# Three pads that move tiles in SBUF, in an encoder layer with a gating unit, a long convolution and a ConvGLU

## The chip, the cores and the metric

The kernel runs on one core of one Trainium2 chip. The metric is the device time of one execution in microseconds, as the median of several runs; less is better. TensorE (PE) multiplies matrices from SBUF into PSUM banks; its weight loads are listed apart, as PEld. VectorE (DVE), ScalarE (ACT) and GpSimd (POOL) do the rest of the arithmetic, SyncE (SP) issues most DMAs. SBUF has 128 partitions; an address here is a byte within a partition.

## The reference

One layer over 512 tokens of width 2048, in float32:

```python
h = rms_norm(x, norm1_g);  p = h @ w_in                      # 2048 -> 5120
zu = gelu(p[:, :1024]);    zv = rms_norm(gelu(p[:, 1024:2048]), sgu_norm_g)
y_a = zu * (sgu_w[head] @ zv + sgu_b)                        # in chunks of 128 tokens
x0, x1, v = dwconv3(p[:, 2048:])                             # three times 1024
u = v * x1;  y_b = x0 * (bidir_long_conv(u, k) + d * u)      # k from a small MLP, through FFTs
x = x + concat(rms_norm(y_a), rms_norm(y_b)) @ w_out
gv = rms_norm(x, norm2_g) @ ffn_w_up                         # 2048 -> 2 * 5504
x = x + (gelu(dwconv3(gv[:, :5504])) * gv[:, 5504:]) @ ffn_w_down
return rms_norm(x, final_g)
```

## The kernel before

Every large product is computed exactly from float32 by three products of a narrower type (`fp32r`): an operand is split into a high part and a rest, `exact_pair` (lines 130 to 132, ScalarE casts, VectorE subtracts), and `mm3` (lines 169 to 172) adds high x high, rest of the moving operand x high, high x rest of the weights into one PSUM bank. `PE.matmul(o, weights, moving)` loads 128 x 128 weights and then streams the moving operand, mostly 512 columns of 4 bytes.

The weights come in units of two K tiles by 512 columns through three buffers each of `raw`, `hi` and `lo` (pool `wp`); `next_unit` keeps the DMA three units and the split two units ahead. The stages, in order:

- projections of h by `w_in` (`projA`, banks `pa`): hi and lo are the weights, hH and hL (the two parts of x times its gain, `split_x`) are moving. 4 feature tiles x 16 K tiles x 3 products are a group of 192 matmuls. For the value branch (`projB`, banks `pv`) the roles are exchanged: hH and hL are weights, hi and lo moving.
- beside them the filter of the long convolution (`filter_pieces`; banks `fh`, `fw`, `fx`; tiles of the pool `mlp`, called `fm`) and the spatial gating unit (`sgu_pieces`, banks `sg`).
- the long convolution in four chunks (`forward`, `products`, `spectra`, `inverse`; banks `fw`, `iv`) woven into the first half of the output projection (`out_group`, banks `po`). Moving there are yh and ylo, the two parts of the gated branch, and in the second half ybH and ybL.
- the FFN in 11 groups of four feature tiles (the last of three): gate and value projections of h2H and h2L (banks `pa`, function `hk` gives the tile), then the down projection (`down`, banks `pd`) with aH and aL moving. Its four blocks of 48 matmuls use the same four banks, which VectorE empties into `xacc` (line 1048). The last group is done in token halves (banks `pl`, 256 columns).

The order is the one in which the code is written, on every engine. A tile's address comes from its pool: pools on the left are stacked upwards from the bottom of SBUF, pools on the right downwards from the top. Left are `const`, `wp`, then in the stack `left` the pool `yl` (au, then ylo; line 220) and, once the filter's pools are closed, `y` (line 647: u and ybH; zH, zL, x0 and ybL; yh). Right are `A` (hH, hL), later `long`, and `A2` and `A3` (h2H, h2L). When `left` is closed, the pool `ffn` (aH, aL) begins where `yl` began.

Of the kernel before, what the change touches and what calls it, by code (L numbers as in the profile page):

```python
# [12 lines left out]
F32 = mybir.dt.float32  # L13
# [4 lines left out]
P = 128  # L18
# [12 lines left out]
CC = 256  # L31
# [11 lines left out]
def encoder_kernel(ctx: ExitStack, tc: tile.TileContext, a: dict, out: bass.AP):  # L43
# [16 lines left out]
    def bank(name):  # L60
        """one of the four banks of the streamed products"""
        return psum.tile([P, 512], F32, tag="mm", name=name, bufs=4)

    def sbank(name):
        """one of the four banks of everything that runs between them"""
        return psum.tile([P, 512], F32, tag="sd", name=name, bufs=4)
# [9 lines left out]

    # ---------------------------------------------------------------- the stream of weights
    # a unit: rows k0*128.. of a weight, nk K tiles by nc_ columns
    plan = []
# [22 lines left out]
    for g in range(2):  # L102
        plan_proj(w_in, 2 * CB + g * 512, 4)
    # beside the long convolution half of the low parts are computed on Pool
    on_pool = set()
# [12 lines left out]
    def load_raw(key):  # L118
        src, k0, nk, c0, n = key
        raw = wp.tile([P, 2, 512], F32, tag="raw", name="raw", bufs=3)  # L120
        rows = src[k0 * P : (k0 + nk) * P, c0 : c0 + n].rearrange("(k p) c -> p k c", p=P)
        if st_["dma"] == 0:
            # the first one in halves, as the products wait for it
            for k in range(nk):
                SP.dma_start(raw[:, k : k + 1, :n], rows[:, k : k + 1, :])
        else:
            SP.dma_start(raw[:, :nk, :n], rows)
        return raw
# [27 lines left out]
    def next_unit(key):  # L156
        """the exact fp32r pair of the next unit; the two after it are already on their way"""
        i = st_["use"]
        assert plan[i][1:] == key[1:] and plan[i][0] is key[0], (i, key)
        split_to(i + 3)  # L160
        dma_to(i + 4)
        st_["use"] += 1
        return split_units.pop(i)
# [9 lines left out]

    # ---------------------------------------------------------------- x and constants
    right = ExitStack()
# [42 lines left out]

    left = ExitStack()
    ylp = pool("yl", stack=left)  # L220

# [3 lines left out]
    def rsqrt(r, ss, n):  # L225
        """r = (ss / n + eps) ** -0.5"""
        DVE.tensor_scalar(r, ss, 1.0 / n, EPS, ALU.mult, ALU.add)
        POOL.tensor_tensor(r, r, nhalf.broadcast_to(list(r.shape)), ALU.pow)

    def rms_col(acc, n, name):  # L230
        """squares, to be summed over the partitions too -> 1/rms, [token, 1] per tile of tokens"""
        nt = acc.shape[-1] // P
        o = sbank("mc")
        for t in range(nt):
            PE.matmul(o[:, t : t + 1], acc[:, t * P : (t + 1) * P], ones[:, 0:1], start=True, stop=True)
        r = const.tile([P, NT], F32, tag="rc", name=name, bufs=3)
        rsqrt(r[:, :nt], o[:, :nt], n)
        return r

    def row_of(r, name, nt=NT):  # L240
        """[token, 1] columns -> the same row of tokens on all partitions"""
        o = sbank("mr")
        for t in range(nt):
            PE.matmul(o[:, t * P : (t + 1) * P], r[:, t : t + 1].broadcast_to([P, P]), ident, start=True, stop=True)
        row = const.tile([P, L], F32, tag="rb", name=name, bufs=2)
        ACT.copy(row[:, : nt * P], o[:, : nt * P])
        return row
# [22 lines left out]

    # ---------------------------------------------------------------- implicit filter
    khat_d = dram.tile([NCC, P, 4 * 2 * CC], F32, name="khat_d")
# [5 lines left out]
    zT, fw1 = zw[:, :L], zw[:, L:]  # L278
    # the last layer comes out twice, on both halves of the partitions
    fw2 = fm.tile([FO, 3 * FO], F32, name="fw2")  # L280
# [23 lines left out]

    # features of the lags: rows 0..63 the high parts, 64..127 the low parts
    h3 = fm.tile([P, L], F32R, name="h3")
    h0 = fm.tile([P, P], F32R, name="h0")

    def mlp_out():
        h = hcur[-1]  # L310
        t = fm.tile([P, L], F32R, name="h3t")
        ACT.copy(t, h)
        ACT.copy(h3[:FO, :], h[:FO, :])
        DVE.tensor_tensor(h3[FO:, :], h[FO:, :], f32(t[FO:, :]), ALU.subtract)
        # the backward half has no tap at lag 0
        DVE.tensor_copy(h0, f32(h3[:, :P]))
        DVE.tensor_scalar(h0[:, 0:1], f32(h0[:, 0:1]), 0.0, None, ALU.mult)
# [5 lines left out]
    def forward_mm(cs, tab, rH, rL):  # L323
        """cos (0) or sin (1) sums of the four token phases [tok, CC] -> banks [128, 2, CC] of phases 0 1, 2 3"""
        Hs, Ls = tab
# [10 lines left out]
    def butterfly(G, U, T):  # L336
        """phase sums (U: 0+2, 1+3; T: 0-2, 1-3) [P, cs, 2, CC] -> frequencies f + 256 j:
        G[:, i, cs, m] holds j = 2 i + m"""
        DVE.tensor_tensor(G[:, 0, :, 0, :], U[:, :, 0, :], U[:, :, 1, :], ALU.add)
# [12 lines left out]
    def filter_pieces(tab):  # L352
# [31 lines left out]
        for c in range(NCC):  # L384
# [35 lines left out]

            # the sum of both directions goes with cos and their difference with sin;
            # the odd phases, which the frequencies f + 256 and f + 768 turn by a quarter, need both
            def turned(cs, tab, rH, rL):
# [45 lines left out]

    # ---------------------------------------------------------------- projections  # L470
    def projA(src, c0, nf, done, rhs=None):
        """[feature, token] tiles of h @ src[:, c0 : c0 + nf*128]; done(ps) takes them out of the banks"""
        ps = [bank("pa") for _ in range(nf)]
# [31 lines left out]

    # value branch, [token, feature]
    gv = [[None] * 2 for _ in range(NT)]
# [23 lines left out]
    def eo(ap):  # L531
        """[P, 512] stored by token modulo 4, seen in token order"""
        return ap.rearrange("p (r m) -> p m r", r=4)
# [3 lines left out]

    # centred depthwise convolutions over tokens (free axis)
    def conv3(pl, ps, r, names, fb, to=None):
        """to: where the result goes, by token modulo 4; without it, in token order in a passing tile"""  # L540
        w0, w1, w2_, b = (lambda i, n=n: col(*n(fb + i)) for n in names)
# [47 lines left out]
    def go_to(n):  # L589
        """emit the products up to K tile n of the projections"""  # L590
        while pos[0] < n:
            next(main)
            pos[0] += 1

    # a_u, with the rest of x and the filter behind its K tiles
    fgen = filter_pieces((tabH, tabL))
# [48 lines left out]
    fs.close()  # L645

    yps.append(pool("y", stack=left))
    yp = yps[0]
    ms = ExitStack()
    mp = pool("mix", side="right", stack=ms)  # L650
    go_to(47)
    # spatial gating weights, transposed: [j, h, i]
    sb = mp.tile([P, NH, P], F32, name="sb")
# [109 lines left out]

    # ---------------------------------------------------------------- long conv and output projection
    keep = ExitStack()
# [41 lines left out]
    def turn(c):  # L807
        """[channel, token] -> [token, channel] pair of u"""
        H, Lo = spl("uH"), spl("uL")
# [182 lines left out]

    # ---------------------------------------------------------------- ConvGLU
    fst = ExitStack()
# [74 lines left out]

    # ---------------------------------------------------------------- the last group, and the final norm  # L1070
    # token halves, so that the first half leaves while the second is computed
    a2s.close()
# [35 lines left out]
    def rms3():  # L1108
        """1/rms per token from tiles of squares"""
        ms_ = [sbank("ms") for _ in range(nt)]  # L1110
# [16 lines left out]
    for th in range(2):  # L1127
        hs = slice(th * HW, (th + 1) * HW)
        # sums of squares: two running ones; at the end the last tiles go to the tensor engine as they are
        accs = [lp_.tile([P, HW], F32, tag=f"ss{i}", name=f"ss{i}", bufs=2) for i in range(2)]  # L1130
# [41 lines left out]
def shape_constants():  # L1172
    """Tables that depend on the sequence length and widths alone."""
    perm = np.concatenate([np.arange(r, L, 4) for r in range(4)])
# [10 lines left out]
    win = np.ascontiguousarray(win.reshape(NT, P, CB).transpose(1, 0, 2))  # L1185
    # transforms of 1024 points at frequencies f + 1/2: forward [m, r, cos/sin, f] for token 4 m + r,
    # inverse [f, parity e, cos/sin, kt, (q m)] for frequency f + 256 kt and token 4 m + 2 q + e
    i = np.arange(P)
# [9 lines left out]

# the vectors that are used as per-partition columns, in one array
_VECS = [  # L1200
# [19 lines left out]
def laid_out(inputs, zT):  # L1220
    """The inputs as the kernel reads them: the same numbers, some of them transposed or packed."""
    g = {n: np.ascontiguousarray(inputs[n]) for n in _INS}
# [30 lines left out]
```

## Time and profile before

| | us |
|---|---|
| median of 3 runs | 2259.96 |
| lowest and highest run | 2259.07, 2260.71 |
| span of the profiled execution, from its first to its last instruction | 2257.4 |
| TensorE busy in it | 2189.7 |
| VectorE, ScalarE, GpSimd busy | 1133.1, 671.9, 317.5 |
| mean granted TensorE clock | 0.982 |

The profiled execution is told by its span; the runs were timed apart from it. A listed duration of a matmul runs from its start to a modelled end and overlaps the next matmul, so a sum of durations is no time; the distance of two starts is. "Idle" is time of an engine before an instruction, with what ended it.

### The profile page before, as it was taken

Reading aid. Unit: us, or ns where it says so; the run is one execution under the profiler, and the core shown is the slowest. Engines: PE = TensorE matmul, PEld = TensorE weight load, DVE = VectorE, ACT = ScalarE, POOL = GpSimd, SP = SyncE. Lnnn points to the kernel's source line nnn. Section 1 sums busy time; section 2 is a strip of 40 time slices with the busy share of each in tenths; the row PEclk is TensorE's granted clock in tenths of the full one; section 3 lists DMA queues with packets and bytes.
Section 4 is the critical chain, followed back from the end, with each engine's and each line's share of the span. In section 5 each row is a group of like instructions: output and inputs, shape, how many; then the busy total and the mean of one; then the engine's idle time right before and its main releaser. Section 6 shows DMA issues by size and latency. Waiting matters only on the chain.

```text
span 2257.4 us, 23811 instructions
## 1 busy us (share of the span) xinstructions
PE 2189.7 (97%) x9742; PEld 1782.5 (79%) x9742; DVE 1133.1 (50%) x1320; ACT 671.9 (30%) x851; POOL 317.5 (14%) x201
## 2 busy tenths in 40 slices
PE   7999999999888999999999999999999999999997
PEld 5778887778777888787887878878787887878877
DVE  8664465556676853534336353443534335343456
ACT  5333432222343332222122221222222122221333
POOL 5221121001344520101001010000101001010003
PEclk9999999999898999999999999999999999999998
DMA  6333223243212423222322323222222222222332
GB/s 208 99 109 122 85 87 92 83 131 111 86 66 93 140 93 96 93 92 94 102 95 93 94 92 95 91 96 94 94 92 95 93 94 93 93 94 85 95 120 75
DMA packets 113480, 223.10 MB, mean 99 GB/s; under 512 B 7035, under 2 KB 18491, under 8 KB 111580
## 3 DMA queue, kind: packets, MB, share of 16 engines
q1 hardware_dynamic: 109184, 215.69, 29.5%
q10 hardware_dynamic: 4188, 5.90, 0.8%
q8 instruction: 76, 1.25, 0.2%
q14 instruction: 32, 0.26, 0.0%
HBM read 213.18 MB, written 8.39 MB: 98 GB/s over the span
## 4 chain that ended last, share of the span: by engine, by line
PE 84%; DVE 10%; issue 2%; POOL 1%; DMA 1%; ACT 1%; SPq 0%; DVEq 0%; POOLq 0%; ACTq 0%
PE pa L170 19%; PE pa L172 19%; PE pa L171 19%; PE pd L170 5%; PE pd L172 5%; PE pd L171 5%; DVE cv L559 2%; DVE lo L132 1%; PE po L170 1%; PE po L171 1%; PE po L172 1%; PE pv L170 1%; PE pv L171 1%; PE pv L172 1%; DVE ev L546 1%
## 5 line engine op out<-in xcount | busy, mean ns | idle before, releaser
L132 DVE TENSOR_TENSOR lo<-raw,hi 128x1024 fp32r<-128x1024 f32 (+2 forms) x369 | 462.6, 1256 | 899.5 <-ACT hi L131 899.4
L131 ACT CAST hi<-raw 128x1024 fp32r<-128x1024 f32 (+2 forms) x369 | 382.3, 1036 | 1156.1 <-PE pa L171 738.2
L170 PE MATMUL pa<-h2H,hi 128*128 128x512 f32 x1376 | 543.6, 395 | 0.0
L172 PE MATMUL pa<-h2H,lo 128*128 128x512 f32 x1376 | 543.4, 395 | 0.0
L171 PE MATMUL pa<-h2L,hi 128*128 128x512 f32 x1376 | 543.4, 395 | 0.0
L172 PEld LDWEIGHTS pa<-h2H,lo 128*128 128x128 f32 x1376 | 258.4, 188 | 62.5
L170 PEld LDWEIGHTS pa<-h2H,hi 128*128 128x128 f32 x1376 | 258.4, 188 | 62.4
L171 PEld LDWEIGHTS pa<-h2L,hi 128*128 128x128 f32 x1376 | 258.4, 188 | 62.4
L170 PE MATMUL pd<-aH,hi 128*128 128x512 f32 x640 | 249.8, 390 | 14.8 <-DVE xacc L1048 14.8
L172 PE MATMUL pd<-aH,lo 128*128 128x512 f32 x640 | 249.2, 389 | 0.0
L171 PE MATMUL pd<-aL,hi 128*128 128x512 f32 x640 | 249.1, 389 | 0.0
L1011 POOL TENSOR_TENSOR gg<-gg,r 128x512 f32<-128x512 f32 x43 | 73.9, 1723 | 1243.8 <-ACT gg L1010 1243.8
L172 PE MATMUL pa<-hH,lo 128*128 128x512 f32 x512 | 206.2, 403 | 6.0 <-DVE lo L132 6.0
L170 PE MATMUL pa<-hH,hi 128*128 128x512 f32 x512 | 207.5, 405 | 1.2 <-DVE ev L546 1.2
L171 PE MATMUL pa<-hL,hi 128*128 128x512 f32 x512 | 205.8, 402 | 0.0
L170 PEld LDWEIGHTS pd<-aH,hi 128*128 128x128 f32 x640 | 120.1, 188 | 43.6 <-ACT hi L131 17.2
L172 PEld LDWEIGHTS pd<-aH,lo 128*128 128x128 f32 x640 | 120.1, 188 | 25.1
L171 PEld LDWEIGHTS pd<-aL,hi 128*128 128x128 f32 x640 | 120.1, 188 | 24.9
L1048 DVE TENSOR_TENSOR xacc<-xacc,pd 128x512 f32<-128x512 f32 x160 | 106.0, 685 | 42.4 <-PE pd L172 42.4
L172 PEld LDWEIGHTS pa<-hH,lo 128*128 128x128 f32 x512 | 98.7, 193 | 32.7 <-DVE lo L132 8.1
L170 PEld LDWEIGHTS pa<-hH,hi 128*128 128x128 f32 x512 | 99.0, 193 | 29.1 <-DVE ev L546 4.2
L171 PEld LDWEIGHTS pa<-hL,hi 128*128 128x128 f32 x512 | 98.6, 193 | 22.0
(243 smaller groups left out, 2305.1 us busy)
## 6 DMA issues: line engine op xcount, KB each, us to landing
raw<-in_ffn_w_up SPq DMA_DIRECT2D x160, 512.0 KB, 3.5
raw<-in_ffn_w_down SPq DMA_DIRECT2D x84, 512.0 KB, 3.5
raw<-in_w_in SPq DMA_DIRECT2D x79, 512.0 KB, 3.6
raw<-in_w_out SPq DMA_DIRECT2D x32, 512.0 KB, 3.5
raw<-in_ffn_w_up SPq DMA_DIRECT2D x16, 384.0 KB, 3.2
khat_d<-kh SPq DMA_DIRECT2D x4, 1024.0 KB, 3.9
kh<-khat_d SPq DMA_DIRECT2D x4, 1024.0 KB, 4.8
res<-in_xT SPq DMA_DIRECT2D x4, 1024.0 KB, 4.7
```

Of the source, the lines that this page charges most:

```text
L131: ACT.copy(hi, src)
L132: eng.tensor_tensor(lo, src, f32(hi), ALU.subtract)
L170: PE.matmul(o, ah, bh, start=start, stop=False)
L171: PE.matmul(o, ah, bl, start=False, stop=False)
L172: PE.matmul(o, al, bh, start=False, stop=stop)
L546: DVE.tensor_tensor(eo(e), pairs(o), pairs(r), ALU.mult)
L559: DVE.scalar_tensor_tensor(dd, e[:, from_ : from_ + z_ - a_], w(f), dd, ALU.mult, ALU.add)
L1011: POOL.tensor_tensor(g_, g_, r2[0], ALU.mult)
L1048: DVE.tensor_tensor(x_, x_, o, ALU.add)
```

## The change

The change opens three pools that nothing reads or writes:

```diff
+    def pad(name, nbytes, side=None, stack=None):
+
+        pool(name, side=side, stack=stack).tile([P, nbytes // 4], F32, name=name)
+
+    pad("padr", 1152, "right")
     right = ExitStack()
     Apool = pool("A", side="right", stack=right)
...
     left = ExitStack()
+    pad("padl", 32, stack=left)
     ylp = pool("yl", stack=left)
...
     fs.close()
 
+    pad("padu", 32, stack=left)
     yps.append(pool("y", stack=left))
```

The rest of the diff drops comments and docstrings, so line numbers shift. `padr` stays for the whole program: every tile on the right lies 1152 bytes lower. `padl` and `padu` live as long as the stack `left`, up to the FFN: `yl` and the filter's tiles lie 32 bytes higher, `y` and what is stacked on it 64 bytes. `const` and `wp` stay, and so do the tiles of `ffn`, which is opened after `left` is closed. On every engine the same instructions stand in the same order. Four waits name another instruction, because tiles of a later pool cover other old ones: VectorE's for the rest part of the inverse table (invL), ScalarE's for its first squares after the residual sum, and GpSimd's for the second and third product of gg.

Where the operands of the matmuls start, in bytes modulo 512 (a weight tile is taken in steps of 512 bytes, a moving tile in steps of 1024 or 2048, so this is the same for each matmul of a row):

| matmul | moving, before | weights, before | moving, after | weights, after |
|---|---|---|---|---|
| pa from hH, hL | 480 | 352 (hi, lo) | 352 | 352 |
| pv | 352 (hi, lo) | 480 (hH, hL) | 352 | 352 |
| po from yh | 352 | 352 (hi, lo) | 416 | 352 |
| po from ylo | 352 | 352 (hi, lo) | 384 | 352 |
| po from ybH, ybL | 352 | 352 (hi, lo) | 416 | 352 |
| pa from h2H, h2L | 480 | 352 (hi, lo) | 352 | 352 |
| pd from aH, aL | 352 | 352 (hi, lo) | 352 | 352 |
| pl (256 columns) | 352 (aH, aL) | 480 (lH, lL) | 352 | 352 |
| iv (256 columns) | 352 (invH, invL) | 480 (sH, sL) | 416 | 352 |
| fw in the convolution (256) | 480 (uH, uL) | 352 (tabH, tabL) | 352 | 416 |
| fw, fx in the filter (256) | 352 (kH, kL) | 352 (tabH, tabL) | 384 | 384 |
| sg (256) | 480 (w2) | 352 (zH, zL) | 352 | 416 |

Modulo 2048, 480 is 2016 for hH, hL, h2H and h2L, and 352 is 864 for hi, lo, aH, aL, yh, ylo, ybH and ybL and, after, for hH, hL, h2H and h2L. Of the pool `y` the yh tiles end at byte 127840 before; h2H3, the lowest h2 tile, starts at 126944, and the other h2 tiles lie between 135136 and 196576.

## Rows read from the trace of the kernel before

**Rows 1.** The page: busy time by engine; the chain that ended last, by engine.
```profile
PE 2189.7 (97%) x9742; PEld 1782.5 (79%) x9742; DVE 1133.1 (50%) x1320; ACT 671.9 (30%) x851; POOL 317.5 (14%) x201
...
PE 84%; DVE 10%; issue 2%; POOL 1%; DMA 1%; ACT 1%; SPq 0%; DVEq 0%; POOLq 0%; ACTq 0%
```

**Rows 2.** Windows: stretch, its us; busy us and instructions by engine; clock, DMA, GB/s.
```profile
0.00:47.00 47.00, 34.09 (x111) 22.90 (x112) 41.05 (x42) 30.90 (x47) 27.93 (x20) 0.93 0.66 230
...
564.00:717.00 153.00, 128.50 (x650) 111.04 (x650) 98.16 (x109) 58.96 (x71) 59.13 (x36) 0.88 0.22 77
966.50:1055.50 89.00, 89.00 (x383) 71.58 (x382) 26.77 (x29) 19.54 (x21) 0.00 (x0) 1.00 0.30 95
332.00:532.00 200.00, 198.35 (x848) 158.99 (x847) 105.83 (x136) 57.17 (x64) 13.66 (x8) 1.00 0.33 102
```

**Rows 3.** Groups of TensorE by form: names, shape, count; busy us, mean ns; idle before.
```profile
L170 PE MATMUL pa<-h2H,hi 128*128 128x512 f32 x1376 | 543.6, 395 | 0.0
...
L170 PE MATMUL pd<-aH,hi 128*128 128x512 f32 x640 | 249.8, 390 | 14.8 <-DVE xacc L1048 14.8
...
L170 PE MATMUL fw<-kH,tabH 128*128 128x256 f32 x32 | 9.0, 282 | 0.0
L170 PE MATMUL fw<-uH,tabH 128*128 128x256 f32 x32 | 9.0, 281 | 0.0
```

**Rows 4.** Instructions on the tile hi: duration ns min/median/max; first and last start us.
```profile
L170 PE MATMUL pa<-h2H,hi x1376: 390/393/478, 785.5 to 2157.3; 128*128 128x512 f32 x197
...
L170 PE MATMUL pd<-aH,hi x640: 387/389/468, 921.2 to 2202.3; 128*128 128x512 f32 x160
```

**Rows 5.** Timeline of TensorE in the FFN: start us, duration us, instruction, idle before.
```profile
1068.60 0.47 PE L170 MATMUL pd<-aH,hi 128*128 128x512 f32 x1 [1.57 <-DVE xacc L1048]
1068.91 0.40 PE L171 MATMUL pd<-aL,hi 128*128 128x512 f32 x1
...
1101.36 0.40 PE L170 MATMUL pa<-h2H,hi 128*128 128x512 f32 x1
...
1190.95 0.39 PE L170 MATMUL pd<-aH,hi 128*128 128x512 f32 x1
```

**Rows 6.** Timeline of TensorE: first and last start of an unbroken run in other stages.
```profile
198.54 0.39 PE L171 MATMUL pv<-lo,hH 128*128 128x512 f32 x1
...
251.06 0.40 PE L172 MATMUL pv<-hi,hL 128*128 128x512 f32 x1
...
399.44 0.40 PE L171 MATMUL pa<-hL,hi 128*128 128x512 f32 x1
...
443.59 0.40 PE L172 MATMUL pa<-hH,lo 128*128 128x512 f32 x1
...
585.43 0.39 PE L170 MATMUL po<-yh,hi 128*128 128x512 f32 x1
...
601.57 0.39 PE L172 MATMUL po<-yh,lo 128*128 128x512 f32 x1
```

**Rows 7.** Timeline of TensorE: 24 matmuls of 256 columns, and the one behind.
```profile
576.90 0.29 PE L170 MATMUL iv<-invH,sH 128*128 128x256 f32 x1
...
579.79 0.40 PE L170 MATMUL po<-yh,hi 128*128 128x512 f32 x1
```

**Rows 8.** Waits of TensorE: who for whom; us in total, times, longest us.
```profile
PE pd L170 <- DVE xacc L1048: 14.8, 10, 1.6
PE iv L170 <- ACT sH L131: 14.4, 4, 4.3
```

## The prediction

> **What bounds the kernel now.** I read the page's busy line and chain first, then the windows by stage, then the groups of matmuls, and last the start times of single matmuls. TensorE is busy 97% of the span and carries 84% of the chain that ended last [rows 1]. By stage [rows 2] only two stretches are not TensorE's: the first 47 us (it is busy for 34.1 of 47 us while x and the first weights arrive) and the long convolution, 564 to 717 us (128.5 of 153 us; the clock is at 0.88 of full there because of the idle spells). In the projections TensorE is busy throughout, at full clock in the two windows shown, while VectorE and ScalarE are at 53% and 29% (332 to 532 us) or 30% and 22% (966.5 to 1055.5 us), and DMA at about 30%. So what counts is the pitch of the matmuls, from one start to the next. No instruction is added, removed or moved by this change; only addresses move.
>
> The pitch is not one number. I take it from start times, since the listed duration of a matmul overlaps the next one. In the FFN [rows 5] the 384 projection matmuls (two groups of 16 K tiles x 4 feature tiles x 3) from 1101.36 to 1190.95 us take 89.59 us, 233.3 ns each. In the down projection the 143 steps from 1068.91 to 1101.36 us take 32.45 us, 226.9 ns each. Shape, type, weights' buffers and clock are the same. The other stages fall into the same two classes [rows 6]: pv, 226 steps, 52.52 us, 232.4 ns; pa from hH and hL, 190 steps, 44.15 us, 232.4 ns; po from yh and ylo, 71 steps, 16.14 us, 227.3 ns. The groups repeat it in durations [rows 3]: 395 ns for h2, 390 ns for aH.
>
> What separates the classes is the layout (the table ahead of the rows). The weight loaded during a matmul is the next one's. Where the moving tile and that weight start at the same byte modulo 512 (aH, aL, yh, ylo, ybH, ybL: 352 and 352), the pitch is 227; where they are 128 bytes apart (hH, hL, h2H, h2L: 480 against 352), it is 232 to 233. pv is the useful row: there hi and lo are moving and hH, hL are the weights, so the distance is the other way round, and it is slow too. Distance inside SBUF is no explanation: the yh tiles end at byte 127840 and the tile h2H3 starts at 126944, and the h2 matmuls, from four tiles spread over 70 KB, have a minimum of 390 and a median of 393 ns against 387 and 389 for aH [rows 4].
>
> **The right pad, 1152 bytes.** 1152 is 2 x 512 + 128, so every tile on the right falls by 128 modulo 512, from 480 to 352: the place of the weights. (Modulo 2048 too: 864, which is where hi, lo, aH, yh and ybH start before.) My step is that these matmuls take the pitch of the equal class.
> - FFN projections: 4128 matmuls (3 x 1376 [rows 3]). 233.3 - 227.0 = 6.3 ns each, 26.0 us. All lie on TensorE's path: the stage has no idle of TensorE but ten waits of 1.6 us at most in the down projection, for VectorE's additions into xacc [rows 8]. Those are counted from the gate's last matmul on, and pitch there does not change (aH and aL stay where they are), so I keep them.
> - Projections from hH, hL: 1536 matmuls, of which 105 lie in the first 47 us (111 matmuls less the small MLP's [rows 2]) and are paced by arrivals; those I count at nothing. The others: 1431 x (232.4 - 227.2), 5.2 ns, is 7.4 us. I take 227.2 as it lies between pd's 226.9 and po's 227.3.
> - pv: 384 x 5.2 is 2.0 us.
> - Matmuls of 256 columns (fw, fx, sg, iv, pl) show no two classes: fw with kH (equal) lasts 282 ns and with uH (128 apart) 281 ns [rows 3]. I count them at nothing. If they followed the others, 288 pl matmuls at 6 ns would be 1.7 us more or less.
>
> Sum: 26.0 + 7.4 + 2.0 = 35.4 us.
>
> **The two left pads, 32 bytes each.** They take yl by 32 and the tiles of y by 64 out of the equal place: ylo comes to 384 (32 past the weights), yh, ybH and ybL to 416 (64 past). ff, with aH and aL, is opened after both are closed, and stays. No row shows a distance of 32 or 64. The nearest rows are 0 (227) and 128 (233.3). From below: 24 matmuls of 256 columns from 576.90 to 579.79 us [rows 7] have a pitch of 120.4 ns, so 256 more columns cost 226.9 - 120.4 = 106.5 ns, and 512 columns alone 213; a pitch cannot go below that, 14 ns under the class of 227. How many matmuls does it touch? The 384 from ybH and ybL nearly all. Of the 384 from yh and ylo, TensorE runs six of every eight K tiles between forward and inverse of a chunk, and then waits up to 4.3 us for sH [rows 8]; a longer or shorter pitch vanishes in that wait. One quarter, 96, counts. So 480 matmuls at -14 to +6.3 ns: -6.7 to +3.0 us. I take half of the upper end, 3.2 ns, as 64 lies half way to 128: +1.5 us.
>
> The filter's tiles (fm on the left) move by 32 together, weights and moving alike. Four waits name another instruction, as tiles of later pools cover other neighbours: one of VectorE's for invL, ScalarE's first squares of norm2, and PoolE's second and third gg product. Each names work that ended many instructions earlier on a queue that is not late there, so: nothing. If one of them did hold, a single wait of TensorE has been at most 4.3 us [rows 8].
>
> **Sum.** -35.4 + 1.5 = -33.9 us. The profiled execution spans 2257.4 us, so 2223.5; the median of the runs is 2.6 us over that span, so 2226.1.
>
> **A rule against it.** In the traces two pitches stand beside each other at the same clock [rows 5, 6]. The Trainium skill (SBUF — State Buffer, Who interferes with whom) says that TensorE has one read port for the moving operand and another for weight loads, independent, and that it never waits on anyone; by that rule the addresses can't matter and the time stays 2260, as in the first rival below. The trace speaks against the rule as far as it reaches, since nothing else that I find separates 227 from 233.
>
> **Rivals.**
> - Addresses are not the cause. Then the down and output projections are fast for another reason (they add up 4 or 8 K tiles, not 16), and nothing changes: 2260. For it: every fast row is also a short accumulation. Against it: nothing in a matmul says how many more follow into the same bank, and po (8 K tiles) and pd (4) are alike though their lengths differ. The independent ports of the section above would give the same. 0.08.
> - Partly given back: in the stages from hH, VectorE and ScalarE also run the filter, the gating and the short convolutions, and TensorE's shorter units wait for hi and lo instead. The windows leave room (53% of VectorE's time at most in a long stretch there), but if all 9.4 us of hH and pv went, the time is 2226.1 + 9.4 = 2236. 0.06.
> - Slower: equal starts collide on the right. The streams of a matmul and of the weight load behind it then touch the same bytes modulo 512 together, and aH and yh are fast because of something else (they lie below byte 128 K, as the weights do, and most of the right-hand tiles lie above it). If that costs one more step of the size seen, 6.3 ns on 4128 + 1536 + 384 = 6048 matmuls is 38.1 us, 2298 us. It decides from a pitch of h2 above 233.3. Against it: h2H3 lies at the border and is as slow as the rest. 0.06.
>
> **How the numbers follow.** The forecast, that right-hand operands take the pitch of 227, gets 0.80; 2226 is its time. Its own spread is the left pads (-6.7 to +3.0 about the +1.5 taken: 2218 to 2228), the size of the hH term (1431 matmuls by 4 to 6 ns, 1.5 us either way), and 256-column matmuls (2 us). The range should reach the second rival: 2216 to 2238, which holds 0.86 less what I may have wrong in the spread. A difference of 0.2%, 4.5 us, is about what can be told from no change in this kernel. Faster: the forecast and the second rival, 0.86; same: the first rival, 0.08; slower: the third, 0.06.
>
> **What would show it.** The FFN projections' 384 matmuls between two down projections should take 87.2 us, not 89.6, and the listed duration of pa from h2 fall from 395 to about 389 ns. pa from hH and pv should go to 227. po from ybH shows what a distance of 64 does: 227 is no effect, 230 what I took. pd must stay at 227, with its waits of 1.5 us. If pa from h2 stays at 233 while po moves, the residue counts in another way than I read; if neither moves, addresses don't count. A pitch of about 213 to 216 in po would put the time at the lower end.

## The result, and the profile after

| | median us | runs |
|---|---|---|
| before | 2259.55 | 2259.07 to 2260.71 |
| with the three pads | 2224.57 | 2222.41 to 2224.85 |

The ratio is 0.9842, with a 95% interval of 0.9828 to 0.9856: 35.0 us less. The forecast was 2226, in a range of 2216 to 2238. The profiled execution spans 2223.0 us, 34.4 less than before. The mean granted clock of TensorE in it is 0.982, as before.

The page after, as [rows 1] and [rows 3] of before: busy time by engine, then groups with the mean duration in ns after the comma.

```profile
PE 2156.4 (97%) x9742; PEld 1782.2 (80%) x9742; DVE 1131.3 (51%) x1320; ACT 671.9 (30%) x851; POOL 312.5 (14%) x201
...
L170 PE MATMUL pa<-h2H,hi 128*128 128x512 f32 x1376 | 535.5, 389 | 0.0
...
L170 PEld LDWEIGHTS pa<-h2H,hi 128*128 128x128 f32 x1376 | 258.3, 188 | 53.6
...
L170 PE MATMUL pd<-aH,hi 128*128 128x512 f32 x640 | 249.8, 390 | 15.3 <-DVE xacc L1055 15.3
```

The counts of instructions, and the busy time of the weight loads and of ScalarE, are those of before; TensorE is busy 33 us less. The matmuls from h2 last 389 ns in place of 395, and pd stays at 390. So the matmuls of the slow class became shorter, with the work around them unchanged.

Now the pitch, from the timeline of TensorE after: first and last start of an unbroken run, in pairs (start us, duration us, instruction).

```profile
196.06 0.40 PE L171 MATMUL pv<-lo,hH 128*128 128x512 f32 x1
...
247.30 0.39 PE L172 MATMUL pv<-hi,hL 128*128 128x512 f32 x1
...
392.85 0.40 PE L171 MATMUL pa<-hL,hi 128*128 128x512 f32 x1
...
435.94 0.39 PE L172 MATMUL pa<-hH,lo 128*128 128x512 f32 x1
...
576.07 0.40 PE L170 MATMUL po<-yh,hi 128*128 128x512 f32 x1
...
592.50 0.40 PE L172 MATMUL po<-yh,lo 128*128 128x512 f32 x1
...
708.52 0.39 PE L171 MATMUL po<-ybL,hi 128*128 128x512 f32 x1
...
776.97 0.39 PE L170 MATMUL pa<-h2H,hi 128*128 128x512 f32 x1
...
922.31 0.40 PE L171 MATMUL pd<-aL,hi 128*128 128x512 f32 x1
...
954.75 0.39 PE L170 MATMUL pa<-h2H,hi 128*128 128x512 f32 x1
...
1086.95 0.39 PE L170 MATMUL pa<-h2H,hi 128*128 128x512 f32 x1
...
1173.99 0.39 PE L170 MATMUL pd<-aH,hi 128*128 128x512 f32 x1
```

| run | steps | pitch before, ns | after, ns |
|---|---|---|---|
| pv | 226 | 232.4 [rows 6] | 226.7 |
| pa from hH, hL | 190 | 232.4 [rows 6] | 226.8 |
| po from yh, ylo | 71 | 227.3 [rows 6] | 231.4 |
| po from ybH, ybL | 299 | 226.8 | 228.9 |
| pd | 143 | 226.9 [rows 5] | 226.8 |
| pa from h2 | 384 | 233.3 [rows 5] | 226.7 |

(The 226.8 of before for ybH, ybL is from the same 299 steps of its trace, 717.70 to 785.51 us.) By stage, cut at the first matmul of each, the profiled executions differ so: up to pv 148.1 and 146.4 us; pv to the end of the projections of h 384.5 and 376.9; long convolution and output projection 252.9 and 253.7; FFN up to pl 1417.5 and 1390.9; the rest 54.4 and 55.2. That is -1.7, -7.6, +0.8, -26.6 and +0.8, in sum -34.3 us (34.4 by the rounded spans). The first of the five is no measure of the change: up to pv the profiled execution takes 145.6 us with a right pad of 128 bytes and 149.3 with one of 1152, two kernels with the same pitches.

### The profile page after: what moved, and what is told of

Its sections match the earlier page's. It is cut to its first block, busy times and chain, and to the rows that moved or that the text cites. A ratio compares the mean times of both kernels' runs of the same rounds, so it can differ in the third digit from the quotient of the medians.

```text
span 2223.0 us, 23810 instructions
## 1 busy us (share of the span) xinstructions
PE 2156.4 (97%) x9742; PEld 1782.2 (80%) x9742; DVE 1131.3 (51%) x1320; ACT 671.9 (30%) x851; POOL 312.5 (14%) x201
## 4 chain that ended last, share of the span: by engine, by line
PE 83%; DVE 10%; issue 3%; ACT 1%; POOL 1%; DMA 1%; SPq 0%; DVEq 0%; POOLq 0%; ACTq 0%
PE pa L170 18%; PE pa L172 18%; PE pa L171 18%; PE pd L170 5%; PE pd L171 5%; PE pd L172 5%; DVE cv L565 2%; DVE lo L132 1%; PE po L170 1%; PE po L172 1%; PE po L171 1%; PE pv L170 1%; PE pv L172 1%; PE pv L171 1%; DVE ev L552 1%
## 5 line engine op out<-in xcount | busy, mean ns | idle before, releaser
L170 PE MATMUL pa<-h2H,hi 128*128 128x512 f32 x1376 | 535.5, 389 | 0.0
L171 PE MATMUL pa<-h2L,hi 128*128 128x512 f32 x1376 | 535.3, 389 | 0.0
L172 PE MATMUL pa<-h2H,lo 128*128 128x512 f32 x1376 | 535.3, 389 | 0.0
```

Of the source, the lines that this page charges most:

```text
L170: PE.matmul(o, ah, bh, start=start, stop=False)
L171: PE.matmul(o, ah, bl, start=False, stop=False)
L172: PE.matmul(o, al, bh, start=False, stop=stop)
```

## Experiments

The theory: the pitch of a matmul goes by the distance, modulo some small power of two, between the bytes at which its moving operand and the weight loaded beside it start. Rivals: only the absolute start or the place in SBUF counts; short accumulations are fast; the pads act in another way. Each kernel is the one before with the edit shown, and its name stands behind the heading. A distance is the start of the moving tile less the start of the weight tile.

**Right pad alone (right_only).**

```diff
+    pool("padr", side="right").tile([P, 288], F32, name="padr")
     right = ExitStack()
```

> The right pad of 1152 bytes alone; no left pads. Theory (the pitch of a matmul goes by the distance, modulo 512 bytes, between where its moving operand and the weight loaded beside it start): pa from h2 and hH and pv go to 227 ns as with all three pads, and po from yh, ylo, ybH, ybL stays at 227 to 228 as before instead of 229 to 232; so 0.5 to 1.5 us faster than with all three pads, about 2223.5. Rival (the left pads are needed for the gain): above 2235, with pa from h2 over 230 ns.

Measured: 2221.57 us, ratio 0.9833 (0.9820 to 0.9847). Two groups of it by form (mean ns after the comma):

```profile
L170 PE MATMUL pa<-h2H,hi 128*128 128x512 f32 x1376 | 535.5, 389 | 0.0
...
L171 PE MATMUL po<-ylo,hi 128*128 128x512 f32 x128 | 49.9, 390 | 0.0
```

The right pad carries the whole gain: pa is at 389 as after, and po from ylo is at 390 as before.

**Left pads alone (left_only).**

```diff
     left = ExitStack()
+    pool("padl", stack=left).tile([P, 8], F32, name="padl")
...
+    pool("padu", stack=left).tile([P, 8], F32, name="padu")
     yps.append(pool("y", stack=left))
```

> The two left pads of 32 bytes alone. Theory: pa from h2 stays at 233 ns, pa from hH and pv at 232; po from yh and ylo goes to 231 or 232 and from ybH, ybL to 229, which costs 1 us or less since two thirds of it lies ahead of a wait: 2259.5 to 2261. Rival (the left pads bring a part of the gain): under 2255.

Measured: 2260.57 us, ratio 1.0005 (0.9997 to 1.0014).

```profile
L170 PE MATMUL pa<-h2H,hi 128*128 128x512 f32 x1376 | 543.6, 395 | 0.0
...
L171 PE MATMUL po<-ylo,hi 128*128 128x512 f32 x128 | 50.5, 394 | 0.0
```

The projections stay slow, po becomes slower by 4 ns, and the time cannot be told from before.

**A right pad of 128 bytes (right_128), and all three pads again (all_three).** The pad is `[P, 32]` in place of `[P, 288]`.

> A right pad of 128 bytes alone, in place of 1152. Theory (only the distance modulo 256 counts): the same as 1152 alone, 227 ns for pa from h2 and hH and for pv, 2222 us, ratio 0.983. Rival (the place modulo 1024 or 2048 counts, or the other 1024 bytes do): pa from h2 stays above 230 ns and the time above 2240 us.

> All three pads again, beside the others on one chip. Theory: about 1 us over right_128, since po from yh and ylo is at 231 and from ybH, ybL at 229 instead of 227, and a part of it lies ahead of a wait; 2223 to 2225 us. Rival (the left pads bring a gain): under right_128.

Measured on one chip: 2222.36 us with 128 bytes (ratio 0.9838, 0.9824 to 0.9851), 2222.84 with all three (the same ratio and interval). The remaining 1024 of the 1152 bytes do nothing that can be told apart. The expected 1 us that the left pads cost is not resolved: the intervals cover each other. What the traces show is that the stage from the first po to the FFN takes 252.4 us with 128 bytes on the right and 253.2 with all three, one execution each.

**The fast matmuls made slow (left_all_128).** One pad above the weights' pool moves everything else on the left by 128 bytes, and the right is left alone:

```diff
     dram = pool("dram", space=bass.MemoryType.DRAM)
+    pool("padw").tile([P, 32], F32, name="padw")
```

> No right pad; one pad of 128 bytes above the weights' pool, so that every tile on the left lies 128 bytes from the weights like those on the right: 480 against 352. Theory: the fast matmuls of before become slow, pd from aH, aL and po at 232 to 233; 1440 of pd's 1920 at 6.4 ns (the first block of 48 of each group ends in a wait) and 480 of po: 9.2 + 3.1 = 12.3 us, 2272 us. Rival (pd and po are fast because they add up fewer K tiles, or because their tiles lie low in SBUF): pd stays at 227, 2260 us.

Measured: 2268.37 us, ratio 1.0038 (1.0024 to 1.0052). The group of pd by form:

```profile
L171 PE MATMUL pd<-aH,hi 128*128 128x512 f32 x640 | 253.4, 396 | 12.4 <-DVE xacc L1049 12.4
```

396 ns against 390 [rows 3]; by start times 232.8 on average. So pd is not fast because it adds up few K tiles, nor because aH lies low in SBUF; both are unchanged here. The cost is 8.6 us where 12.3 were expected. The stages of the profiled execution show where it is missing. The FFN up to pl is 6.8 us longer where 9.2 were expected: pd's 1920 matmuls cost 5.8 ns each, 11.1 us, of which 2.4 vanish in the waits for xacc (14.8 [rows 8] to 12.4; the expectation had left 480 matmuls, 3.1 us, out for them), and the matmuls from h2, with unchanged residues, are at 232.7 in place of 233.2 on average (4128 x 0.5 = 2 us). The long convolution and output projection are 1.3 us longer where 3.1 were expected.

The 0.5 ns of h2 has a visible origin. Single steps of the slow class, read from the start times to the ns, are not equal; they follow a repeating pattern, and the distance of 128 bytes has two: steps of 229 and 238 ns by turns (233.3 on average), and a longer sequence with steps from 228 to 241 ns (232.4). Of the 86 blocks of 48 matmuls from h2, 9 had the second pattern before, by their mean, and 53 have it here. It is also the pattern of pv and of most of pa from hH, which is why they stand at 232.4. What selects the pattern is open. At distance 0, after the change, nearly all steps are 226 or 227 ns.

**The distance, scanned (five kernels named dist).** Pads ahead of or inside the four pairs of h2 tiles give each pair a distance of its own, for 48 matmuls in a row. Three kernels put pads between the pairs:

```diff
     def h2_tiles(pl, q):
+        n = (64, 64, 64, 0)[q]
+        if n:
+            pl.tile([P, n // 4], F32, name=f"pad{q}")
         return pl.tile([P, 4, L], F32R, name=f"h2H{q}"), pl.tile([P, 4, L], F32R, name=f"h2L{q}")
```

(with 192 on the right; the others have 32, 32, 32 with 32 on the right, and 192, 32, 32 with 416). Two let the tiles start inside larger ones:

```diff
+        o = (4, 12, 2, 1)[q]
+        ts = [pl.tile([P, 4 * L + 64], F32R, name=f"h2{x}{q}") for x in "HL"]
+        return tuple(t[:, o : o + 4 * L].rearrange("p (k t) -> p k t", k=4) for t in ts)
```

(with 1152 on the right; the other has 15, 14, 12, 8 with 1216).

> No left pads; a right pad of 192 bytes, and pads of 64 bytes between the four pairs of h2 tiles, so that they start -192 (h2H0), -128 (h2H1), -64 (h2H2) and -256 bytes (h2H3) from the weights, modulo 512; hH and hL start at -64. Theory: the four pairs have different pitches inside each group of 192 matmuls; -128 is slow, about 232 to 233, as the distance of pv before; aH stays at 227. If the pattern repeats after 256 bytes, h2H3 is at 227. Rival (only the absolute start of the moving tile counts, or where in SBUF it lies): no clear steps between the four, or steps in the order of the addresses.

> No left pads; a right pad of 32 bytes, and pads of 32 bytes between the pairs of h2 tiles, so that they start +32 (h2H0), +64 (h2H1), +96 (h2H2) and 0 bytes (h2H3) from the weights; hH and hL start at +96. Theory: h2H3 at 227; +64 at 229 or more, as po from ybH has with all three pads (229), and +32 at about 231 as ylo has; +96 up to 233. Rival (only the absolute start counts, or the place): no clear steps.

> A right pad of 416 bytes and pads between the pairs of h2 tiles: distances to the weights of +160 (h2H0), +192 (h2H1), +224 (h2H2) and +480 bytes (h2H3); hH and hL at +224; no left pads. Theory (the pitch goes by the distance with a period of 256 bytes): +192 is at 233.4 like -64, and +480 and +224 are one case, equal to within 0.5 ns and over 229. Rival (the period is 512): +480 and +224 differ.

> The right pad of 1152; the h2 tiles start inside larger tiles, +16 (h2H0), +48 (h2H1), +8 (h2H2) and +4 bytes (h2H3) from the weights, modulo 256. Theory: the pitch goes up within 32 bytes, from 227 at 0 to 233 at 32; +4 and +8 are at 227 to 230 and +16 at 229 to 232; +48 between 229 and 234. Rival (some small distance is better than 0): one of them under 226.

> The same on the other side: -4 (h2H0), -8 (h2H1), -16 (h2H2) and -32 bytes (h2H3); hH and hL at -64. Theory: -32 equals +224, and the pitch goes down to 227 towards 0; hH at 233 as with a distance of -64 before. Rival (a small distance is better than 0): one of them under 226.

In the timeline of a group each pair has 4 K tiles of 12 matmuls; the rows are the first matmul of h2H0, H1, H2, H3 and of the next h2H0, 48 steps apart. First for -192, -128, -64, -256:

```profile
1096.84 0.40 PE L170 MATMUL pa<-h2H,hi 128*128 128x512 f32 x1
...
1107.84 0.40 PE L170 MATMUL pa<-h2H,hi 128*128 128x512 f32 x1
...
1119.00 0.39 PE L170 MATMUL pa<-h2H,hi 128*128 128x512 f32 x1
...
1130.20 0.39 PE L170 MATMUL pa<-h2H,hi 128*128 128x512 f32 x1
...
1141.10 0.40 PE L170 MATMUL pa<-h2H,hi 128*128 128x512 f32 x1
```

11.00, 11.16, 11.20 and 10.90 us for the same 48 matmuls: 229.2, 232.5, 233.3 and 227.1 ns. The same for +32, +64, +96, 0:

```profile
1103.45 0.40 PE L170 MATMUL pa<-h2H,hi 128*128 128x512 f32 x1
...
1114.65 0.40 PE L170 MATMUL pa<-h2H,hi 128*128 128x512 f32 x1
...
1125.65 0.40 PE L170 MATMUL pa<-h2H,hi 128*128 128x512 f32 x1
...
1136.87 0.39 PE L170 MATMUL pa<-h2H,hi 128*128 128x512 f32 x1
...
1147.79 0.40 PE L170 MATMUL pa<-h2H,hi 128*128 128x512 f32 x1
```

233.3, 229.2, 233.8 and 227.5 ns. And for -4, -8, -16, -32:

```profile
1095.02 0.39 PE L170 MATMUL pa<-h2H,hi 128*128 128x512 f32 x1
...
1105.94 0.39 PE L170 MATMUL pa<-h2H,hi 128*128 128x512 f32 x1
...
1117.09 0.39 PE L170 MATMUL pa<-h2H,hi 128*128 128x512 f32 x1
...
1128.43 0.40 PE L170 MATMUL pa<-h2H,hi 128*128 128x512 f32 x1
...
1139.62 0.40 PE L170 MATMUL pa<-h2H,hi 128*128 128x512 f32 x1
```

227.5, 232.3, 236.3 and 233.1 ns. All the distances, as means of start-to-start times over the some 1030 matmuls of each pair in a kernel (steps over 260 ns left out):

| distance, bytes modulo 256 | pitch, ns |
|---|---|
| 0 | 226.7 (after), 227.5 (beside +96) |
| 0, from -256 | 227.1 |
| +4, +8, +16 | 236.9, 233.7, 231.6 |
| +32, +48 | 233.4, 233.2 |
| +64 | 229.1; from -192: 229.2 |
| +96 | 233.6 |
| +128 | 233.2 (before); from -128: 232.4 |
| +160 | 234.2 |
| -64 | 233.4; from +192: 233.3 |
| -32 | 233.2; from +224 and +480: 233.2, 233.3 |
| -16, -8, -4 | 236.2, 232.1, 227.9 |

Distances that differ by 256 give the same pitch within 0.8 ns (the 0.8 is the two patterns at 128 bytes, above), so the pitch repeats after 256 bytes; it does not after 64 (0 and +64 differ) nor after 128 (+64 and -64 differ). Only 0 and -4 have a pitch under 229. The tiles of one kernel lie in the order H3, H0, H1, H2 and the pitch does not follow it, so the place is no cause. The times of the five kernels (2246.53, 2253.30, 2257.19, 2252.50 and 2249.61 us, one run each) are mixtures of these classes.

pv confirms the sign, since the tiles that these pads move are weights there: with hH 64 bytes below hi it has the distance +64 and 229.2 ns, at +160 it has 234.2 and at +32 233.3, each within 0.2 ns of the h2 matmuls at the same distance.

Three expectations were wrong. For small positive distances the pitch does not rise from 0 to 32, it is highest at +4. On the negative side it does not fall steadily towards 0, it rises from 233.2 at -32 to 236.2 at -16 first. And +32 was expected at 231 and has 233.4.

**Own weight or next weight (lo_tile_by_128, hi_tile_by_128).** `lo` alone is moved by 128 bytes, with the right pad; then `hi` alone. The edit for `lo` (for `hi`, the pad `[P, 32]` stands ahead of `hi`, and `[P, 96]` ahead of `lo`):

```diff
+            if i == 0:
+                wp.tile([P, 32], F32, name="padlo")
             lo = wp.tile([P, 2, 512], F32R, tag="lo", name="lo", bufs=3)
+            if i == 0:
+                wp.tile([P, 96], F32, name="padwp")
```

> The right pad of 1152, no left pads, and lo alone moved by 128 bytes against hi, so that moving operands and hi start at the same residue and lo 128 from them. In mm3 the weights are hi, hi, lo. Theory (what counts is the weight that is loaded during the matmul, which is the next one's): line 171, during which lo is loaded, goes from 227 to about 232, lines 170 and 172 stay at 227; about 1.7 ns a matmul on average, 9000 matmuls, 2235 to 2240 us. Rival (its own weight counts): line 172 is the slow one, same time.

> The right pad of 1152, no left pads, and now hi moved by 128 bytes and lo left at the residue of the moving operands: the reverse of lo_tile_by_128, where the two lines that have lo as their own or as the next weight were slow. Theory A (a matmul is slow, by one step, when its own or the next weight lies elsewhere): the first of mm3 (own hi, next hi), the second (hi, lo) and the third (lo, hi) are all slow, 232 to 234 ns, and the time is that of before, 2257 to 2262 us. Theory B (each weight that lies elsewhere costs a fixed sum, wherever it is paid: 13.3 ns a weight by lo_tile_by_128): 26.6 ns over three matmuls, pitches of 680 + 27 = 707 ns for three, over 2275 us. Theory C (cost in proportion to the time in which the two streams differ): two thirds of the matmuls slow, about 2248 us.

Groups by form; lines 174, 175 and 176 are the three of `mm3`, with weights hi, hi, lo. `lo` moved, 2251.56 us (2235 to 2240 expected; one run, as for `hi`):

```profile
L176 PE MATMUL pa<-h2H,lo 128*128 128x512 f32 x1376 | 546.3, 397 | 0.0
L175 PE MATMUL pa<-h2L,hi 128*128 128x512 f32 x1376 | 544.9, 396 | 0.0
L174 PE MATMUL pa<-h2H,hi 128*128 128x512 f32 x1376 | 535.5, 389 | 0.0
```

`hi` moved, 2269.80 us:

```profile
L176 PE MATMUL pa<-h2H,lo 128*128 128x512 f32 x1376 | 546.8, 397 | 0.0
L175 PE MATMUL pa<-h2L,hi 128*128 128x512 f32 x1376 | 543.5, 395 | 0.0
L174 PE MATMUL pa<-h2H,hi 128*128 128x512 f32 x1376 | 540.9, 393 | 0.0
```

Both expectations of the first kernel fell: the matmul whose next weight is lo (175) and the one whose own weight is lo (176) are both slow, 232.5 and 234.2 ns from start to start, and the third stays at 226.7. The down projection repeats it: 226.8, 232.5 and 234.1. In the second all three are slow, 232.4, 232.6 and 235.0, 700 ns together: theory A of the three, and not the 707 of B. In both kernels the moving tiles of pa and pd lie where they lie with the right pad alone, so it is not the absolute start of the moving tile that counts. The time of theory A was put 8 us too low, since the down and output projections, fast before, are slow in this kernel too (as in the kernel with everything on the left moved, +8.6 us).

So in pa and pd it looks as if a matmul paid one step when either its own weight or the next one starts elsewhere, and no second step when both do. As a rule of the hardware this is not shown, and pv of the same two kernels speaks against it. There hi and lo are moving (hi, lo, hi) and all weights stay at one residue, so the rule gives one slow matmul of three, some 686 ns together, with `lo` moved, and two, some 692, with `hi` moved. First and last start of 222 steps in each, `lo` moved first:

```profile
194.68 0.40 PE L174 MATMUL pv<-hi,hH 128*128 128x512 f32 x1
...
246.47 0.40 PE L174 MATMUL pv<-hi,hH 128*128 128x512 f32 x1
...
194.97 0.39 PE L174 MATMUL pv<-hi,hH 128*128 128x512 f32 x1
...
245.78 0.39 PE L174 MATMUL pv<-hi,hH 128*128 128x512 f32 x1
```

That is 700 ns for three with `lo` moved and 687 with `hi` moved, the other way round. The first 21 steps of pv with `lo` moved took 687, with the same residues. Nor can a single step be charged to a single weight, since steps of equal matmuls differ by 9 ns and more (229 and 238 by turns, above): a delay in one may come out in the next. That rival, in which only the weight loaded during a matmul counts and the matmul behind it inherits a part, is untested. What is shown is that the weight tiles' starts count, all of those that a loop alternates between, and not how the cost falls on single matmuls. The trace lists a weight load as 188 of the 227 ns, with idle time behind it (the row of PEld after, above). What the hardware does there stays open.

## Why the prediction was right, point by point

- **The pitch, read from start times, as the thing that counts, and two classes of it by residue.** Right. In the scan, an equal start is the class of 227 and 128 bytes apart that of 232 to 233, wherever the tile lies, and left_all_128 turned the fast class slow.
- **FFN projections, 26.0 us.** The stage is 26.6 us shorter (27.7 to 28.4 in right_only, right_128 and all_three): 4128 matmuls from 233.2 to 226.7 on average. Between two down projections the 384 take 87.04 us, where 87.2 were forecast, and pd stays at 226.8.
- **hH, hL and pv, 7.4 + 2.0 us.** By the pitches, 232.5 to 227.3 for pa and 232.4 to 227.0 for pv, the terms were sized right (7.4 and 2.1 us). The stages up to the output projection, 9.3 us shorter, agree in part by luck, since the time up to pv varies by some 4 us between the right-pad kernels. No new wait took the place, which speaks against the second rival; TensorE's waits after (who for whom, us in total, times, longest):

```profile
PE pd L170 <- DVE xacc L1055: 15.3, 11, 1.6
PE iv L170 <- ACT sH L131: 13.5, 4, 4.1
PE iv L172 <- DVE sL L132: 8.8, 4, 2.4
PE pa L172 <- DVE lo L132: 6.6, 5, 3.1
```

  The first two stood at 14.8 and 14.4 before [rows 8], the wait for lo at 6.0.
- **256-column matmuls, nothing.** They have no classes of 6 ns, but they are not blind to the distance either: the median pitch of fw from u is 120 ns at 128 bytes (before) and at 0 (right_only), and 118 at -64 (after) and +64 (left_only); that of sg goes the same way. On so few matmuls it is worth nothing. From pl's first matmul on, the end is 0.8 us longer after. The same kernel had 54.4 us in its second profile, so that lies within the spread of executions; the 56.1 us with either right pad alone are not explained.
- **The left pads, +1.5 us in a range of -6.7 to +3.0.** The stage grew by 0.8 us. For 64 bytes the value taken, 3.2 ns, was near: 228.9 - 226.8 = 2.1 in po from ybH, ybL. But the reason given, half way to 128, was wrong: the scan goes 227, 233, 229, 234, 233 for 0, 32, 64, 96, 128. yh (+64) and ylo (+32) together pay 4.1 ns a matmul, more than the 64 bytes alone, which the working did not see; the scan's pitches, 229.1 twice and 233.4, would give 230.5 on average, and 231.4 was measured. That this cost little is the wait behind them: they grow by 4.1 ns x 72 = 0.3 us between forward and inverse of a chunk, and TensorE's wait for sH fell from 14.4 [rows 8] to 13.5 us. It is 14.3 and 14.4 with a right pad alone, and 13.4 with the left pads alone and with all three a second time.
- **The independent read ports.** The sum by that rule, no change, fell with the result. The Trainium skill (SBUF — State Buffer, Who interferes with whom) has TensorE wait on no one; in these runs a distance between its two operands changes the pitch of 512 columns by 1 to 10 ns, so here the measurement decides against the sentence, whatever the cause inside.
- **The four moved waits, nothing.** None shows up in TensorE's waits; of those above, none differs from before by more than 0.9 us.
- **The sum.** The span was forecast at 2223.5 and is 2223.0 us. Of the 1.5 us between the forecast median and the measured one, 1.0 is the step from span to median, taken as 2.6 us from the runs before and 1.6 after. That both fit so well is in part luck: runs of one kernel differ by 1.6 to 6.3 us.
- **The rivals.** The first fell with right_only, where h2 with its 16 K tiles is at 226.7, and with left_all_128; the third fell with h2 at 227.

The right pad alone carries the gain, by 128 of its bytes, as the steps had it. The fastest version is that one pad (2222.36 us, or 2221.57 with 1152 bytes); with the left pads the difference is not measurable.

## What to carry to other kernels

When two groups of matmuls of one shape and type have different pitches at the same clock, compare where their operands start in SBUF. Here equal starts modulo 256 bytes of the moving tile and of every weight tile that it meets gave 227 ns for 512 columns of 4 bytes, and nearly every other distance 229 to 237 (256 columns did not follow this); a pad of 128 bytes was worth 1.6% of the whole kernel. Check all operands of a loop, since one of two alternating weight tiles at another residue already slowed two of three matmuls.

## What was not expected of the hardware

- The best distances are narrow: 0 has 226.7 to 227.5 ns and -4 has 227.9, but -8 has 232.1, and +4 is the worst of all with 236.9. The pattern is not symmetrical (+64: 229.1, -64: 233.4).
- With lo alone moved, the matmul that uses lo slowed in pa as well as the one before it (234.2 and 232.5 ns); which load causes which delay is not shown.
- One distance can have more than one pitch: at 128 bytes equal matmuls run at 229 and 238 ns by turns (233.3) or in a longer pattern (232.4).
- Matmuls of 256 columns have no step between 0 and 128 bytes (fw from uH lasted 281 ns at 128 and from kH 282 at 0 [rows 3]), but a median pitch of 118 ns at -64 and +64, against 120.
